# Where a second stream's steps are put among the loads of sixteen experts

## The chip, the cores and the metric

The kernel runs on one core of a Trainium2 chip. The metric is device time of one execution, in microseconds (us). In what follows TensorE does the matrix products, VectorE (DVE in the profile) and ScalarE (ACT) the elementwise work, GpSimd (POOL) some elementwise work and loads, SyncE (SP) only issues loads. PE is TensorE's matmul row in the profile, PEld its weight loads.

## The reference

The reference chains two blocks over one sequence of 256 tokens of width 1024, all in fp32. The first block is attention followed by a mixture of 16 experts; the second has two layers, and its first layer also updates a second sequence, the context, of 256 tokens. What matters here is the expert part and the context's share of the second block's first layer:

```python
def run_expert(args):                       # 16 times; each expert takes its 32 best tokens
    wg, wu, wd, ie, ge = args               # wg, wu: 1024 x 2816, wd: 2816 x 1024
    xe = h[b_rows, ie]
    he = jax.nn.silu(xe @ wg) * (xe @ wu)
    return (he @ wd) * ge[..., None].astype(h.dtype)
...
hc = ctx * (1 + csc1) + csh1                # the context, layer 0
y, yc = _mla_mixer(h, hc, ...)              # 8 heads of attention, low-rank projections
ctx = _layer_norm(alpha * ctx + cg1 * yc, ln1_g[i], ln1_b[i])
ctx = _layer_norm(alpha * ctx + cg2 * _mlp(ctx * (1 + csc2) + csh2, mlp_w1[i], mlp_w2[i]), ...)
```

The context's work does not depend on the experts' results, only the later layers need both.

## The kernel before

**Three parts.** `front` does the first attention and the routing, `experts` the sixteen experts, `tail` all that is left of the second block. The context's attention and MLP are written as a generator, `ctx_stream`, and run inside `experts`: each `next` of it issues one step (part of an attention unit, half a hidden chunk of the MLP, half of an output chunk) in the middle of the expert's own instructions. All engines take their instructions in the order in which the program issues them, so where a step is issued decides what waits behind it.

**One expert.** The 32 tokens of an expert are the stationary operand, the weights stream. For each of 8 slices k of the inner dimension, a tile of w_gate and one of w_up (1408 KB each) are taken, and 8 products each go into four banks of PSUM (L955 to L963; in the profile `egg<-wg` and `egu<-wg`, 16 instructions each). Then `Silu` and multiplications (`hh`), transposes (`eht`), copies (`hT`). Then 11 tiles of w_down (1024 KB each) are taken, and 4 products of each go into two banks `py` (L1006 to L1014, `ey<-wd`). At last `py` is copied to `ye`, and products with the routing matrix scatter it (`esc`), which VectorE adds to the result (L1022 to L1030).

**The loads.** `expert_loads` lists all 27 tiles of all experts in order; SP issues them. The class `Loader` gives a tile a buffer out of six (nine for the first expert); the next load is issued when an older tile's last product has been issued (`done`) and waits on the chip for that product. The context's weights (46 loads of up to 1024 KB) come on POOL's queue through a second loader with four buffers.

**PSUM.** There are eight banks: tag "g" has four, given out in pairs in turn (`pair`), tag "d" two, tag "c" two. Gate and up products take a pair of "g" each. `py`, the transposes `eht`, the scatter `esc` and many of the context's products take "d".

**The order around the change.** After each k, from the sixth k of the first expert on, the program issues as many context steps as a count asks for: `want` grows linearly with the number of k done, from `CTX_FROM` to all k but `CTX_LEFT`, up to `steps`. The stream itself has fewer steps than 154; when it is used up, `next` does nothing. Between the tiles of the down products no step is issued. Before the last expert's down products whatever is left is drained (L976).

Of the kernel before, what the change touches and what calls it, by code (L numbers as in the profile page):

```python
# [19 lines left out]
NE = 16  # L20
# [86 lines left out]
PROJ_PULLS = (0, 0, 1, 0, 0, 0, 0)  # L107
ADA_VECTOR = 6
WOUT_AT = (15, 16)
CTX_FROM = 5  # L110
CTX_LEFT = 16


class Loader:
# [39 lines left out]
def drain(gen):  # L154
    for _ in gen:
        pass


class Kernel:
# [764 lines left out]
    def experts(self, es, right, xs, oh, slots):  # L924
        tc, nc, a = self.tc, self.nc, self.a
        le = self.le
        xp = self.pool(es, "xe")
        self.load_tabs(1, xp, nc.gpsimd)
        xeT = xp.tile([128, 8, NE * CAP], F32, name="xeT")

        def gather(k):
            p = self.bank("d", [128, 512], "gat")
            n = 0
            for tt in range(2):
                for t in xs:
                    nc.tensor.matmul(p, t[:, tt, k * 128:k * 128 + 128], oh[:, tt], start=n == 0, stop=n == 3)
                    n += 1
            if k % 2:
                nc.vector.tensor_scalar(xeT[:, k], p, self.col("norm2", k), None, op0=OP.mult)
            else:  # L940
                nc.scalar.activation(xeT[:, k], p, AF.Copy, scale=self.col("norm2", k))
        ctx = None
        steps = 154
        got = 0

        for e in range(NE):
            ps = {n: self.pair("eg" + n[2:3]) for n in ("w_gate", "w_up")}
            if e == 0:
                gather(0)
            for k in range(8):  # L950
                if e == 0 and k < 7:
                    gather(k + 1)
                elif e == 0:
                    slots()
                for n in ("w_gate", "w_up"):  # L955
                    w = le.take((n, e, k))
                    for h in range(2):
                        for j in range(4):
                            c0 = j * FJ + h * 352
                            nc.tensor.matmul(ps[n][h][32 * j:32 * j + 32, :352],  # L960
                                             xeT[:, k, e * CAP:(e + 1) * CAP], w[:, c0:c0 + 352],
                                             start=k == 0, stop=k == 7, skip_group_check=True)
                    le.done((n, e, k))  # L963
                if (e, k) == (0, 4):
                    self.early.close()
                    ew = self.pool(es, "ew")
                    self.sw = self.rows = self.pool(es, "sw")
                    ctx = self.ctx_stream()
                if ctx is None:
                    continue  # L970
                want = steps * (8 * e + k + 1 - CTX_FROM) // (8 * NE - CTX_LEFT - CTX_FROM)
                while got < want:
                    got += 1
                    next(ctx, None)
            if e == NE - 1:
                drain(ctx)  # L976

            hh = ew.tile([128, 2, FJ], F32, name="hh", tag="hy")
            h2 = hh.rearrange("p u (a b) -> p u a b", a=2)
            for h in range(2):  # L980
                nc.scalar.activation(h2[:, 0, h], ps["w_gate"][h][:, :352], AF.Silu)
                for u in (1, 0):
                    nc.vector.tensor_mul(h2[:, u, h], h2[:, 0, h], ps["w_up"][h][:, :352])  # L983

            hT = ew.tile([128, 11, 2, 32], F32, name="hT")
            hr = hh.rearrange("p u (m r) -> p r (u m)", r=11)
            for b in range(3):
                n = (4, 4, 3)[b]
                p = self.bank("d", [128, n, 128], "eht%d" % b)
                for i in range(n):  # L990
                    nc.tensor.transpose(p[:, i], hr[:, 4 * b + i], self.ident)
                pv = p.rearrange("p r (q s t) -> p r q s t", q=2, s=2)
                for s in range(2):
                    f = nc.scalar.copy if s else nc.vector.tensor_copy
                    f(hT[64 * s:64 * s + 64, 4 * b:4 * b + n], pv[64 * s:64 * s + 64, :, :, s])
            if e < NE - 1:
                sg, ye = ew.tile([128, 256], F32, name="sg"), None
            else:
                t = self.s8([128, 2048], "sgye")
                sg, ye, jk = t[:, :256], t[:, 256:256 + D], t[:, 256 + D:768 + D]  # L1000
                nc.scalar.activation(self.warm, self.one, AF.Sqrt)
            nc.vector.tensor_scalar(sg, self.tab("iota"), self.idxg[:, e, 0:1], self.idxg[:, e, 1:2],
                                    op0=OP.is_equal, op1=OP.mult)
            py = [self.bank("d", [128, 512], "ey%d" % h) for h in range(2)]

            for n in range(11):  # L1006
                w = le.take(("d", e, n))
                for h in range(2):
                    for u in range(2):
                        r, q = (2 * (n // 2) + u, n % 2) if n < 10 else (10, u)  # L1010
                        s = 2 * u + (h + n) % 2
                        nc.tensor.matmul(py[h][32 * s:32 * s + 32, :], hT[:, r, q], w[:, u, h * 512:h * 512 + 512],  # L1012
                                         start=n < 2, stop=n >= 9, skip_group_check=True)
                le.done(("d", e, n))  # L1014
                if le.next == len(le.items) and self.lw.hold:

                    self.lw.hold = None
                    self.lw.pump()
            if ye is not None:
                return sg, ye, py, jk  # L1020
            ye = ew.tile([128, D], F32, name="ye", tag="hy")
            nc.scalar.copy(ye[:, :512], py[0])  # L1022
            nc.vector.tensor_copy(ye[:, 512:], py[1])  # L1023
            for tt in range(2):
                for h in range(2):
                    p = self.bank("d", [128, 512], "esc")
                    nc.tensor.matmul(p, sg[:, tt * 128:tt * 128 + 128], ye[:, h * 512:h * 512 + 512],
                                     start=True, stop=True)
                    xs_ = self.x[:, tt, h * 512:h * 512 + 512]
                    nc.vector.tensor_add(xs_, xs_, p)  # L1030
# [1077 lines left out]
```

## Time and profile before

| what | value |
|---|---|
| median of 3 timed runs | 2421.96 us (2421.23 to 2422.09) |
| the profiled execution's own time | 2429.35 us |
| its span, first to last instruction | 2427.5 us |
| mean granted clock of TensorE over the span | 0.87 |
| TensorE busy | 2075.3 us, 85% |
| VectorE busy | 821.8 us, 34% |
| read from memory over the span | 783.23 MB |
| up to 220 us: share of the transfer engines, GB/s | 0.85, 300 |
| 220 to 1655 us | 0.99, 410 |
| 1655 to 2427 us | 0.53, 173 |

How to read the rows of the next section. In the page's part in 40 slices a digit is the busy share of a slice of 60.7 us in tenths. In a table of stretches each row has the stretch, its length, the busy time of PE, PEld, DVE, ACT and POOL with the number of instructions, the granted clock of TensorE (1.00 is 2.4 GHz, 0.50 is 1.2 GHz), the share of time in which the 16 transfer engines were busy, and GB/s. In a timeline each row has the start, the length, engine, source line, what is written and read, the count, and in brackets how long the engine sat idle before it and what ended that. In a list of waits: who waited for whom, total us, times, longest us.

### The profile page before, as it was taken

How to read it: one execution, taken by the hardware profiler on the slowest of the kernel's cores; microseconds unless marked ns; L12 is line 12 of the kernel's file. 1: busy time of each engine (PE TensorE's matmuls, PEld its weight loads, DVE VectorE, ACT ScalarE, POOL GpSimd, SP SyncE). 2: the span in 40 equal slices, each digit the busy share in tenths (PEclk: the TensorE clock that was granted, in tenths of full speed). 3: DMA queues.
4: the chain of work that ended last, by engine and by line, in shares of the span. 5: the costliest groups of instructions: out<-in, count | busy, mean ns of one | idle time of the engine just before them, and what ended most of it. 6: DMA issues, size and time to landing. Idle time of an engine off the chain costs nothing. (4 is left out here: it accounts for less than half of the span.)

```text
span 2427.5 us, 32038 instructions
## 1 busy us (share of the span) xinstructions
PE 2075.3 (85%) x13644; PEld 1255.1 (52%) x13644; DVE 821.8 (34%) x1488; ACT 544.2 (22%) x984; POOL 246.4 (10%) x253
## 2 busy tenths in 40 slices
PE   8998888797898888987777777777998999998998
PEld 7864334332443433533122111114787998987897
DVE  5643112221112111113011001105558765377555
ACT  5432011200000000000000000004444453375443
POOL 2121000001000000000000000003213013133001
PEclk9988898897988988989666666658999999999999
DMA  9788999799999999999999999997537864333652
GB/s 336 259 316 337 410 392 422 292 417 415 411 416 416 413 404 414 414 418 392 423 422 421 422 422 422 420 423 287 204 125 257 271 221 131 101 103 131 206 185 87
DMA packets 179222, 787.59 MB, mean 324 GB/s; under 512 B 13280, under 2 KB 73928, under 8 KB 125576
## 3 DMA queue, kind: packets, MB, share of 16 engines
q1 hardware_dynamic: 154648, 694.96, 72.6%
q0 software_dynamic: 24288, 89.54, 10.2%
q8 instruction: 107, 1.75, 0.3%
q10 hardware_dynamic: 144, 1.05, 0.1%
q14 instruction: 35, 0.29, 0.0%
HBM read 783.23 MB, written 2.27 MB: 324 GB/s over the span
## 5 line engine op out<-in xcount | busy, mean ns | idle before, releaser
L1012 PE MATMUL ey<-wd,hT 128*32 128x512 f32 x1408 | 242.2, 769 | 107.2 <-DMA wd<-in_w_down 107.2
L960 PE MATMUL egu<-wg,xeT 128*32 128x352 f32 x2048 | 228.3, 574 | 61.4 <-DMA wg<-in_w_up 61.3
L378 DVE TENSOR_TENSOR wl<-cwt,wh 128x1024 fp32r<-128x1024 f32 (+1 forms) x202 | 259.9, 1329 | 58.0 <-ACT wh L377 57.8
L960 PE MATMUL egg<-wg,xeT 128*32 128x352 f32 x2048 | 224.8, 567 | 42.5 <-DMA wg<-in_w_gate 42.4
L377 ACT CAST wh<-cwt 128x1024 fp32r<-128x1024 f32 (+2 forms) x218 | 214.6, 1034 | 94.1 <-issue 50.1
L1012 PEld LDWEIGHTS ey<-wd,hT 128*32 128x32 f32 x1408 | 40.4, 123 | 290.8 <-DMA wd<-in_w_down 234.7
L960 PEld LDWEIGHTS egu<-wg,xeT 128*32 128x32 f32 x2048 | 68.4, 127 | 205.4 <-DMA wg<-in_w_up 120.7
L960 PEld LDWEIGHTS egg<-wg,xeT 128*32 128x32 f32 x2048 | 60.8, 124 | 195.3 <-issue 104.7
L173 PE MATMUL ph<-hTxh,wh 128*128 128x256 f32 x512 | 146.0, 285 | 1.5 <-ACT hTxh L1110 1.5
L174 PE MATMUL ph<-hTxl,wh 128*128 128x256 f32 x512 | 145.9, 285 | 0.7 <-DVE hTxl L1113 0.7
L175 PE MATMUL ph<-hTxh,wl 128*128 128x256 f32 x512 | 145.5, 284 | 0.8 <-DVE wl L378 0.8
L983 DVE TENSOR_TENSOR hh<-hh,egu 128x352 f32<-128x352 f32 x64 | 32.4, 519 | 300.3 <-PE egu L960 295.9
L1489 ACT ACTIVATE hu<-ph 128x512 f32<-128x512 f32 x48 | 28.7, 597 | 444.6 <-PE ph L171 340.5
L171 PE MATMUL py<-cwt,hs 128*128 128x512 f32 x256 | 121.1, 620 | 0.0
L171 PE MATMUL ph<-hcT,cwt 128*128 128x256 f32 x512 | 118.1, 385 | 0.0
L1023 DVE COPY ye<-ey 128x512 f32<-128x512 f32 x15 | 10.4, 691 | 315.3 <-PE ey L1012 315.3
L171 PEld LDWEIGHTS ph<-hcT,cwt 128*128 128x128 f32 x512 | 96.0, 191 | 27.6 <-issue 15.1
L173 PE MATMUL acc<-wh,hsh 128*128 128x512 f32 (+1 forms) x256 | 99.3, 388 | 5.9 <-ACT hsh L1497 5.9
L173 PEld LDWEIGHTS ph<-hTxh,wh 128*128 128x128 f32 x512 | 98.4, 192 | 2.7 <-ACT hTxh L1110 2.1
L174 PEld LDWEIGHTS ph<-hTxl,wh 128*128 128x128 f32 x512 | 98.3, 192 | 1.9 <-issue 0.8
L175 PEld LDWEIGHTS ph<-hTxh,wl 128*128 128x128 f32 x512 | 98.4, 192 | 1.0 <-DVE wl L378 1.0
L175 PE MATMUL acc<-wh,hsl 128*128 128x512 f32 (+1 forms) x256 | 98.6, 385 | 0.0
(545 smaller groups left out, 3454.7 us busy)
## 6 DMA issues: line engine op xcount, KB each, us to landing
wg<-in_w_gate SPq DMA_DIRECT2D x128, 1408.0 KB, 17.3
wg<-in_w_up SPq DMA_DIRECT2D x128, 1408.0 KB, 17.9
wd<-in_w_down SPq DMA_DIRECT2D x176, 1024.0 KB, 13.2
cwt<-in_w SPq DMA_DIRECT2D x64, 1024.0 KB, 5.3
cwt<-in_w POOLq DMA_DIRECT2D x32, 1024.0 KB, 14.5
adaw<-in_ada_w SPq DMA_DIRECT2D x24, 1024.0 KB, 8.0
adaw<-in_ada_w POOLq DMA_DIRECT2D x24, 1024.0 KB, 7.6
cwt<-in_w_in SPq DMA_DIRECT2D x12, 1024.0 KB, 10.5
```

The lines of the kernel that those rows point to most:

```text
L171: t.matmul(out, L[0], R[0], start=start, stop=stop, **kw)
L173: t.matmul(out, L[0], R[0], start=start, stop=False, **kw)
L174: t.matmul(out, L[0], R[1], start=False, stop=False, **kw)
L175: t.matmul(out, L[1], R[0], start=False, stop=stop, **kw)
L377: (high or nc.scalar.copy)(parts[0][:, s], t[:, s])
L378: (eng or self.low_eng).tensor_tensor(parts[1][:, s], t[:, s], parts[0][:, s].bitcast(F32), op=OP.subtract)
L960: nc.tensor.matmul(ps[n][h][32 * j:32 * j + 32, :352], xeT[:, k, e * CAP:(e + 1) * CAP], w[:, c0:c0 + 352], start=k == 0, stop=k == 7, ski ...
L983: nc.vector.tensor_mul(h2[:, u, h], h2[:, 0, h], ps["w_up"][h][:, :352])
L1012: nc.tensor.matmul(py[h][32 * s:32 * s + 32, :], hT[:, r, q], w[:, u, h * 512:h * 512 + 512], start=n < 2, stop=n >= 9, skip_group_check=True)
L1023: nc.vector.tensor_copy(ye[:, 512:], py[1])
L1489: nc.scalar.activation(u, p, AF.Relu)
```

## The change

Steps are counted in units of bytes: a k has 11 units (two tiles of 1408 KB), a tile of the down products 4 (1024 KB), an expert 8 x 11 + 11 x 4 = 132. The context starts at the same k as before (unit 55) and is dealt over the units up to the end of the fifteenth expert; 109 steps stand in place of 154 over 107 k. A helper `context` issues what is due after each k and now also after each down tile. The two banks `py` of the down products come from the pairs of tag "g" in place of tag "d".

```diff
-CTX_FROM = 5
-CTX_LEFT = 16
+UNITS = 11, 4, 8 * 11 + 11 * 4
+CTX_FROM = 5 * 11
+CTX_LEFT = 8 * 11 + 11 * 4
+CTX_STEPS = 109
...
         ctx = None
-        steps = 154
         got = 0
+
+        def context(units):
+
+            nonlocal got
+            want = CTX_STEPS * (units - CTX_FROM) // (UNITS[2] * NE - CTX_LEFT - CTX_FROM)
+            while ctx is not None and got < want:
+                got += 1
+                next(ctx, None)
...
                     ctx = self.ctx_stream()
-                if ctx is None:
-                    continue
-                want = steps * (8 * e + k + 1 - CTX_FROM) // (8 * NE - CTX_LEFT - CTX_FROM)
-                while got < want:
-                    got += 1
-                    next(ctx, None)
+                context(UNITS[2] * e + UNITS[0] * (k + 1))
             if e == NE - 1:
                 drain(ctx)
...
-            py = [self.bank("d", [128, 512], "ey%d" % h) for h in range(2)]
+            py = self.pair("ey")
 
             for n in range(11):
                 w = le.take(("d", e, n))
...
                     self.lw.pump()
+                context(UNITS[2] * e + 8 * UNITS[0] + UNITS[1] * (n + 1))
```

## Rows read from the trace of the kernel before

**Rows 1.** The page's 40 slices, the transfer engines.
```profile
DMA  9788999799999999999999999997537864333652
```
**Rows 2.** Table of stretches: two long ones of the expert stage.
```profile
530.00:1120.00 590.00, 507.95 (x2970) 231.22 (x2970) 101.90 (x170) 27.04 (x55) 38.41 (x42) 0.89 1.01 413
...
1200.00:1640.00 440.00, 320.94 (x1946) 82.66 (x1946) 38.74 (x73) 16.29 (x37) 0.00 (x0) 0.64 1.01 422
```
**Rows 3.** Table of stretches of 20 us, those with a share below 0.99.
```profile
240.00:260.00 20.00, 15.04 (x115) 6.06 (x112) 5.67 (x14) 1.98 (x5) 0.00 (x0) 0.83 0.95 384
...
340.00:360.00 20.00, 15.97 (x107) 5.51 (x98) 4.54 (x10) 3.74 (x7) 0.75 (x1) 0.91 0.87 341
...
420.00:440.00 20.00, 16.92 (x123) 12.50 (x124) 4.87 (x17) 5.58 (x18) 0.70 (x1) 1.00 0.82 317
440.00:460.00 20.00, 15.20 (x128) 9.06 (x126) 7.62 (x24) 7.07 (x18) 1.81 (x3) 0.99 0.79 295
460.00:480.00 20.00, 14.42 (x91) 4.40 (x91) 1.75 (x5) 1.05 (x3) 0.00 (x0) 0.84 0.64 257
...
840.00:860.00 20.00, 16.53 (x90) 9.24 (x88) 4.10 (x9) 2.36 (x6) 0.90 (x1) 0.83 0.94 368
...
1140.00:1160.00 20.00, 15.06 (x92) 2.98 (x91) 1.28 (x4) 0.97 (x4) 0.00 (x0) 0.77 0.85 342
```
**Rows 4.** Timeline of TensorE, 395 to 475 us.
```profile
403.81 1.39 PE L960 MATMUL egg<-wg,xeT 128*32 128x352 f32 x16
...
413.95 1.39 PE L960 MATMUL egg<-wg,xeT 128*32 128x352 f32 x16
...
431.25 1.39 PE L960 MATMUL egg<-wg,xeT 128*32 128x352 f32 x16
...
455.04 1.17 PE L1401 MATMUL mpo<-mptS,vc 128*128 128x128 f32 x8
```
**Rows 5.** Waits of SP's queue of loads, 395 to 475 us.
```profile
SPq L909 <- PE egg L960: 28.4, 3, 15.7
```
**Rows 6.** Timeline of TensorE, a tile of the second expert's down products.
```profile
361.37 1.06 PE L1012 MATMUL ey<-wd,hT 128*32 128x512 f32 x8 [1.43 <-DMA wd<-in_w_down]
```
**Rows 7.** Timeline of TensorE, 795 to 862 us, steps of the context's MLP.
```profile
798.87 3.60 PE L171 MATMUL py<-cwt,hs 128*128 128x512 f32 x8
802.40 1.39 PE L960 MATMUL egg<-wg,xeT 128*32 128x352 f32 x16
803.61 1.37 PE L960 MATMUL egu<-wg,xeT 128*32 128x352 f32 x16
...
829.01 2.57 PE L960 MATMUL egu<-wg,xeT 128*32 128x352 f32 x16 [2.98 <-DMA wg<-in_w_up]
```
**Rows 8.** Timeline of TensorE, 1100 to 1165 us, the tenth expert's transposes.
```profile
1138.05 2.96 PE L991 MATMUL eht<-tabs,hh 128*128 128x128 f32 x11 [10.31 <-DVE hh L983]
```
**Rows 9.** Groups of instructions: count, busy us, mean ns, idle before.
```profile
L1023 DVE COPY ye<-ey 128x512 f32<-128x512 f32 x15 | 10.4, 691 | 315.3 <-PE ey L1012 315.3
```
**Rows 10.** Loads by line: queue, count, size, median us from issue to landing.
```profile
cwt<-in_w POOLq DMA_DIRECT2D x32, 1024.0 KB, 14.5
```
**Rows 11.** Table of stretches of 20 us, three more of the expert stage.
```profile
800.00:820.00 20.00, 19.89 (x130) 10.54 (x132) 3.90 (x6) 0.60 (x1) 1.85 (x3) 1.00 1.01 411
...
860.00:880.00 20.00, 13.29 (x47) 3.20 (x48) 2.15 (x4) 0.59 (x1) 0.00 (x0) 0.66 1.02 423
...
1340.00:1360.00 20.00, 15.41 (x96) 3.58 (x96) 0.00 (x0) 0.00 (x0) 0.00 (x0) 0.51 1.01 423
```
**Rows 12.** Table of stretches of 5 us, 830 to 860 us.
```profile
830.00:835.00 5.00, 5.00 (x16) 1.71 (x9) 0.00 (x0) 0.00 (x0) 0.00 (x0) 0.50 0.99 398
835.00:840.00 5.00, 5.00 (x40) 2.06 (x39) 1.37 (x2) 0.00 (x0) 0.70 (x1) 0.99 1.01 418
...
850.00:855.00 5.00, 4.94 (x21) 2.63 (x25) 1.50 (x4) 1.05 (x3) 0.00 (x0) 0.50 0.92 350
855.00:860.00 5.00, 4.97 (x42) 1.11 (x34) 0.00 (x0) 0.00 (x0) 0.00 (x0) 0.94 0.81 284
```

## The prediction

> **What bounds the kernel now.** I read the page's forty slices first. The transfer engines stand at 9 tenths in every slice from the fifth to the twenty-seventh but one, which is at 7 [rows 1]: this is the expert stage, about 220 to 1650 us. After it the transfers are light. So I took the expert stage apart, and asked where the transfer engines rest in it, since nothing else can shorten a stretch that they fill.
>
> Two long stretches give the terms. From 1200 to 1640 us no context step is left: share 1.01, 422 GB/s, TensorE busy 320.94 of 440 us at a mean granted clock of 0.64 [rows 2]. From 530 to 1120 us experts and context run together: share 1.01 again, 413 GB/s, TensorE 507.95 of 590 us at 0.89. Both are full of transfers. (A share of 1.01 is what the view shows of engines that never rest.) TensorE has slack in both, but little in the second.
>
> Then I went through the stage in stretches of 20 us and kept those whose share is below 0.99: there are seven [rows 3]. Lost time is (1.01 - share) x 20 us: 1.2 at 240, 2.8 at 340, 3.8, 4.4 and 7.4 from 420 to 480, 1.4 at 840, 3.2 at 1140, together 24.2 us. That is all that any new order of the same work can win in this stage. The bytes stay the same.
>
> Why the engines rest is seen best at 403 to 460 us [rows 4]. The gate products of five k begin at 403.81, 413.95, 431.25, ... and the last context products end at 456.2: 52.4 us for five k. One k's pair of tiles is 2 x 1408 KB, 2.88 MB, or 6.8 us at 422 GB/s; five need 34 us. TensorE is the late one, because the context takes its turn in there. The queue of loads says the same: in this window SP's loads of down tiles waited 28.4 us for gate products to free a tile, once for 15.7 us [rows 5]. There are six tiles: when TensorE falls more than their worth behind, nothing can be loaded. In the down phase it is the other way round: TensorE waits for each tile, 1.43 us before products of 1.06 us, 2.49 us a tile [rows 6]. So the stage has a phase with too much for TensorE and one with too little, and six tiles can't carry the difference where the context's steps are heaviest.
>
> **The change part by part.** *The dealing.* The context stream has 108 yields (4 + 24 + 8 + 4 + 1 + 64 + 2 + 1 by the code), so a count of 109 spends it all. Before, 154 steps were dealt over 107 k: 1.44 a k, all in the gate and up phase, spent at the end of the tenth expert. After, 109 steps go over 1925 units: a k (11 units) gets 0.62, a down tile (4 units) 0.23, an expert 7.5, spent at the end of the fifteenth. The units are right by bytes: 2.88 / 1.05 MB = 2.75 = 11 / 4.
>
> TensorE's need against the transfers', at the full clock. The gate and up products of one k take 2.6 us (1.39 and 1.37, overlapping) and a step of the context's MLP 3.6 to 3.7 us [rows 7]. In the heavy attention stretch a step costs (52.4 - 5 x 2.6) / 7.2 = 5.5 us, 7.2 being 5 x 1.44. Per k that was 2.6 + 1.44 x 5.5 = 10.5 us against 6.8 of transfers; it becomes 2.6 + 0.62 x 5.5 = 6.0 us. In the MLP 2.6 + 1.44 x 3.65 = 7.9 becomes 4.9 us, against 6.8 plus about 0.8 for the context's own half load a step. In the down phase 1.06 becomes 1.06 + 0.23 x 3.65 = 1.9 us (attention: 2.3), against 2.5. TensorE is thus ahead of the transfers everywhere, and the six tiles (15 to 20 us of transfers) cover a single long step (the k from 413.95 to 431.25 held two in 17.3 - 2.6 = 14.7 us, so some 9 for the longest [rows 4]) and the pause before the down products.
>
> The rests at 340, 420 to 480 and 840 us should go, 19.8 us. The one at 1140 has another cause: the last norm of the context runs as one block on VectorE in front of the expert's, and the transposes wait 10.31 us [rows 8]. Now its two halves fall some 1.6 k, or six down tiles, apart, so I count its 3.2 us as won too. The one at 240 us lies in the first expert with its gathers; fewer context steps fall there (2 for 4), so it may lose all or nothing of 1.2; I leave it. That gives 23.0 us.
>
> *The sums in other banks.* The down sums take the pair of banks of the gate products, which are read before the transposes, and the next up products take those of the down sums. They must wait for the copies of the sums, but the scatter products ahead of them in TensorE's order wait for those already. Cost nothing, 0.7 us an expert at worst (the copy, 691 ns [rows 9]), covered anyway by the loaded tiles. The two banks freed are what lets a context step run between down tiles; its evacuation, of the same size, must be over when the scatter wants the bank: again 0.7 us an expert at most, under the same cover.
>
> *The context's loads.* The same 46 loads on POOL's queue, each asked for when an older tile is done, four tiles ahead. A tile lasts two MLP steps, so four last over an expert, 82 us (8 x 6.8 + 11 x 2.49), against 14.5 us to land [rows 10]: none is late. The rate over a long stretch is 413 GB/s with them and 422 without [rows 2]: a price of their bytes, which I keep at no change. If it were a price of the stream being alive, five more experts of it, 410 us, at 2% (422 to 413) would cost 9 us; inside the first stretch it is 411 GB/s at 800 us, among context steps, and 423 at 860, in a down phase [rows 11], which speaks against, so 0.
>
> *What may come new.* The clock. Before 829 us TensorE waited 2.98 us for a tile [rows 7]; in the next 5 us the granted clock read 0.50, the slower level, while TensorE was 5.00 of 5.00 us busy, and then 0.99. It had fallen behind, and at 850 to 860 the share fell to 0.92 and 0.81: 1.45 us lost [rows 12]. After the change TensorE is ahead of the transfers more often, so it waits and slows more often. At the slower level the gate and up products take 15.41 of 20 us [rows 11], 5.3 us a k, and a step up to 7.3. Bounds: none of these rests, or one of 1.45 us in each of the 8.6 experts that hold the MLP's 64 steps, 12.5 us. The plain cause at 850 was two steps in one k on top of it, which the new dealing rules out, so I take the near end: two of them, 3 us.
>
> Sum: 23 - 3 = 20 us won. The tail is a chain of other work that starts when the stage ends, so it moves forward whole. Against the profiled execution, 2429.35 us, that is 2409.3; it runs 7.4 us above the median of the three timed runs, so by their median 2421.96 - 20 = 2402 us.
>
> **Rivals.** *The clock takes half of it.* One rest of 1.45 us in each expert: 23 - 12.5 = 10.5 won, 2411.5 us. For it: the slower level in the down phases and everywhere from 1200 us [rows 2, 11]. Against: a step every 1.6 k leaves 2 us of slack a k at full clock.
>
> *Slower: the clock stays down and TensorE becomes the bound.* An expert with its share of context needs 8 x 2.6 + 11 x 1.06 + 7.5 x 3.65, about 60 us at full clock, plus about 10 us of waits at the turn to the down products; its transfers 38.5 MB / 413 GB/s = 93 us. It decides where 60 / clock + 10 = 93, at a mean clock of 0.72, between the 0.89 with the context and the 0.64 without. At 0.64 the expert would take 104 us, 11 more; over 8.6 experts 95 us lost, 72 with the rests won: 2494 us. Against it: a TensorE without pauses is what brought 0.99 back within 5 us at 835 [rows 12], so a lag heals itself. The Trainium skill (Perfetto Trace Analysis, section Matmul Optimizations) says that the matmul engine scales with utilization and that matmuls should be issued back to back in batches; by that rule thinning the context out is a loss, and this rival is its case. The trace agrees as far as the clock goes, 0.89 in the denser stretch and 0.64 in the thinner, but not that time was lost at 0.64: transfers were full there.
>
> *The rests only move.* The attention steps still come in lumps, or VectorE's part of a context step stands before an expert's turn to the down phase, and as much is lost elsewhere: 2422 us. Against: the lag that empties the tiles needs several heavy steps within 20 us, and they are now 1.6 k, 11 us, apart.
>
> **How the numbers follow.** All or nearly all of the 24.2 us: 0.68, 2402 us, with a range of its own from 2397 to 2407. Half: 0.18, 2411.5. Moves only: 0.07. Slower: 0.07. A difference of 0.2%, 4.8 us, is about what a measurement of this kernel tells from no change. So faster 0.86, same 0.07, slower 0.07. The range for 8 in 10: 2396 (all rests and a little of the rate) to 2414 (the half case with a bit more lost).
>
> **What would show it.** Right: in 20 us stretches the share stays at 1.0 from 260 to about 1630 us; the last context work ends near 1550; SP's waits for gate products shrink; the stage ends 20 us earlier, the tail has the same length. TensorE's mean clock in the stage lies between 0.64 and 0.89. Wrong: stretches with share under 0.95 at the slower level after 500 us (the clock), or at the turns to the down products (VectorE), or a rate under 410 GB/s at a full share over long stretches (the loads).

## The result and the profile after

The changed kernel takes 2402.19 us (median of four runs, 2398.96 to 2403.98) against 2422.03 us for the kernel before: a ratio of 0.9916, with a 95% interval from 0.9899 to 0.9934. The profiled execution took 2403.98 us, 25.4 less than that of before, which stood 7.3 above the median given here.

The first view is again the page's 40 slices, the transfer engines. The slice that stood at 7 in [rows 1] is full.

```profile
DMA  9788999999999999999999999997537864334652
```

Tables of stretches of the kernel after, columns as in [rows 2]: two long ones, then the places of 20 us where the rests were [rows 3], and all three with a share below 0.99.

```profile
530.00:1120.00 590.00, 454.07 (x2865) 183.33 (x2864) 88.58 (x160) 30.24 (x66) 26.88 (x27) 0.87 1.01 415
...
1200.00:1540.00 340.00, 264.32 (x1668) 109.42 (x1660) 57.77 (x99) 17.56 (x34) 8.80 (x12) 0.87 1.01 414
...
240.00:260.00 20.00, 15.18 (x105) 5.28 (x102) 5.89 (x14) 1.97 (x5) 0.00 (x0) 0.83 1.01 420
...
440.00:460.00 20.00, 17.45 (x102) 8.03 (x102) 5.22 (x11) 3.87 (x8) 0.00 (x0) 0.93 1.01 422
460.00:480.00 20.00, 15.27 (x126) 9.01 (x118) 2.60 (x9) 2.38 (x7) 0.71 (x1) 1.00 1.01 420
...
1060.00:1080.00 20.00, 15.92 (x81) 8.18 (x82) 4.66 (x10) 2.36 (x6) 0.90 (x1) 0.83 0.96 377
...
1340.00:1360.00 20.00, 16.83 (x79) 7.70 (x75) 4.79 (x10) 1.05 (x3) 0.70 (x1) 0.82 0.96 386
...
1440.00:1460.00 20.00, 16.15 (x104) 8.05 (x105) 3.94 (x9) 1.05 (x3) 0.00 (x0) 0.91 0.98 385
```

By the prediction's measure, (1.01 - share) x 20 us, the rests fell from 24.2 to 2.6 us. TensorE's clock, 0.89 and 0.64 in [rows 2], is 0.87 in both stretches (the second ends at 1540 us here, near the end of the context's work).

Two instructions that every version has make a ruler: the first gather product of the first expert, and ScalarE's copy of the last expert's down sums. Between them lie 1446.9 us before (208.3 to 1655.2) and 1424.1 after (208.3 to 1632.4): 22.8 us less, against 21.6 us fewer rests. What comes behind is 772.3 and 769.8 us.

How it looks on TensorE: the heaviest attention stretch of the kernel after, timeline of TensorE, columns as in [rows 4].

```profile
471.75 1.39 PE L970 MATMUL egg<-wg,xeT 128*32 128x352 f32 x16
...
481.90 1.39 PE L970 MATMUL egg<-wg,xeT 128*32 128x352 f32 x16
...
484.29 1.37 PE L970 MATMUL egg<-wg,xeT 128*32 128x352 f32 x16
487.96 1.39 PE L970 MATMUL egu<-wg,xeT 128*32 128x352 f32 x16 [2.30 <-DMA wg<-in_w_up]
...
523.47 3.64 PE L1017 MATMUL ey<-wd,hT 128*32 128x512 f32 x32
...
529.69 1.16 PE L1407 MATMUL mpo<-mptS,vc 128*128 128x128 f32 x8
530.78 2.78 PE L1017 MATMUL ey<-wd,hT 128*32 128x512 f32 x24
```

The k that begins at 471.75 has a step and lasts 10.2 us; the next, at 481.90, has none; the one after it finds its up tile not there yet and waits 2.30 us for the transfer. TensorE has caught up. And at 523.47 four down tiles are followed by attention products before the next three: work that stood in the gate and up phase before.

### The profile page after: what moved, and what is told of

Read it like the earlier page. It is cut to its first block, busy times and chain, and to the rows that moved or that the text cites. A ratio compares the mean times of both kernels' runs of the same rounds, so it can differ in the third digit from the quotient of the medians.

```text
span 2402.2 us, 32033 instructions
## 1 busy us (share of the span) xinstructions
PE 2013.8 (84%) x13644; PEld 1247.1 (52%) x13644; DVE 820.2 (34%) x1488; ACT 551.5 (23%) x990; POOL 245.2 (10%) x253
## 3 DMA queue, kind: packets, MB, share of 16 engines
q0 software_dynamic: 24288, 89.54, 10.2%
## 4 chain that ended last, share of the span: by engine, by line
PE 44%; DMA 40%; DVE 5%; ACT 2%; issue 1%; DVEq 0%; ACTq 0%; SPq 0%
DMA wg<-in_w_up 28%; DMA wd<-in_w_down 10%; PE egu L970 4%; PE ey L1017 4%; PE py L174 3%; PE acc L176 3%; PE acc L178 3%; PE acc L177 3%; PE ph L178 2%; PE ph L177 2%; PE ph L176 2%; DMA wg<-in_w_gate 2%; PE egg L970 2%; PE nqkv L176 2%; PE nqkv L177 2%; PE nqkv L178 2%
## 5 line engine op out<-in xcount | busy, mean ns | idle before, releaser
L970 PE MATMUL egu<-wg,xeT 128*32 128x352 f32 x2048 | 217.8, 551 | 115.0 <-DMA wg<-in_w_up 115.0
L1017 PE MATMUL ey<-wd,hT 128*32 128x512 f32 x1408 | 200.9, 680 | 83.0 <-DMA wd<-in_w_down 82.9
L970 PE MATMUL egg<-wg,xeT 128*32 128x352 f32 x2048 | 202.2, 518 | 63.0 <-DMA wg<-in_w_gate 63.0
L1516 DVE TENSOR_TENSOR accc<-accc,py 128x512 f32<-128x512 f32 x60 | 41.3, 688 | 282.9 <-PE py L174 282.9
L174 PE MATMUL py<-cwt,hs 128*128 128x512 f32 x256 | 131.7, 661 | 0.0
L174 PE MATMUL ph<-hcT,cwt 128*128 128x256 f32 x512 | 129.3, 409 | 0.0
L174 PEld LDWEIGHTS ph<-hcT,cwt 128*128 128x128 f32 x512 | 102.3, 206 | 43.0 <-issue 28.8
L1498 DVE SCALAR_TENSOR_TENSOR hs<-ph,hu 128x512 f32<-128x512 f32 x16 | 11.1, 692 | 297.4 <-ACT hu L1495 297.4
L307 POOL DMA_DIRECT2D cwt<-in_w x32 | 25.7, 803 | 802.8 <-PE ph L174 332.7
```

The source lines that it names most:

```text
L174: t.matmul(out, L[0], R[0], start=start, stop=stop, **kw)
L307: q.dma_start(v, src)
L970: nc.tensor.matmul(ps[n][h][32 * j:32 * j + 32, :352], xeT[:, k, e * CAP:(e + 1) * CAP], w[:, c0:c0 + 352], start=k == 0, stop=k == 7, ski ...
L1498: nc.vector.scalar_tensor_tensor(h, p, 0.0, u, op0=OP.max, op1=OP.mult)
L1516: nc.vector.tensor_add(s, s, p)
```

## The experiments

Each was run beside the kernel before on the same chip. Stage is the ruler above, and rests the sum of (1.01 - share) x 20 us over the stretches below 0.99 from 220 us to the stage's end; both are of the one profiled execution.

| run | median us | ratio to before (95%) | stage us | rests us |
|---|---|---|---|---|
| before | 2422.03 | | 1446.9 | 24.2 |
| the change | 2402.19 | 0.9916 (0.9899 to 0.9934) | 1424.1 | 2.6 |
| banks alone | 2417.66 | 0.9978 (0.9965 to 0.9991) | 1443.1 | 19.4 |
| 15 experts, k only, old banks | 2415.42 | 0.9967 (0.9952 to 0.9982) | 1439.8 | 15.0 |
| the same, new banks | 2410.53 | 0.9949 (0.9935 to 0.9963) | 1438.8 | 14.6 |
| the change, 10 experts | 2409.03 | 0.9942 (0.9927 to 0.9956) | 1431.4 | 9.4 |
| runs of 8 KB | 2390.11 | 0.9864 (0.9849 to 0.9878) | 1415.7 | 2.8 |
| runs of 2 KB | 2396.81 | 0.9890 (0.9867 to 0.9912) | 1417.5 | 1.4 |
| turn | 2400.86 | 0.9910 (0.9888 to 0.9932) | 1424.4 | 2.0 |
| turn and 2 KB | 2395.56 | 0.9889 (0.9866 to 0.9913) | 1420.8 | 4.2 |
| limit of five | 2400.22 | 0.9900 (0.9870 to 0.9930) | 1423.3 | 2.4 |
| five buffers | 2424.56 | 1.0016 (0.9995 to 1.0036) | 1446.7 | 8.8 |

The median of the kernel before in the three later sittings was 2421.83 to 2423.74 us. In the eight rows in which neither the loads' runs nor the number of buffers differ, stage less rests is 1420.9 to 1424.8 us: the rests alone account for the differences, within 4 us. In the three rows with longer runs it is 1412.9, 1416.1 and 1416.6 us.

**The banks alone** (in the kernel before):

```diff
-            py = [self.bank("d", [128, 512], "ey%d" % h) for h in range(2)]
+            py = self.pair("ey")
```

> The kernel before with the down sums in the pairs of tag g alone, dealing as before. Theory (the lag of TensorE makes the rests): nothing changes, 2422 us within 3, and the share of the transfer engines still falls at 420 to 480 us by the same 15 us or so. Rival (the banks themselves are part of the gain, since transposes, scatter and context products no longer queue for two banks): 5 to 15 us faster than before.

Some 5 us by the ratio, in an interval that leaves out 1: the theory missed it, and the rival's lowest figure is what was measured. TensorE's weight loads had a wait that went away. Waits of TensorE's weight loads in the kernel before, 220 to 1655 us: who waited for whom, us in all, times, longest.

```profile
PEld ey L1012 <- ACT hT L995: 14.8, 28, 0.7
```

The down sums took the banks that the last transposes were being copied from, so the first down product waited twice an expert for a copy of which its operands don't need the result; with banks of their own that wait is gone from the list. That is about 1 us a turn. The list alone doesn't show a gain, since the idle time without a releaser (`issue`) before the same weight loads grew from 40.0 to 104.8 us. The timelines of both runs do: at the five turns where the transfers rested before, the products of the first down tile end 0.2 to 1.4 us sooner after the first transpose. The rests are 4.8 us less in all.

**Fifteen experts, no steps between down tiles** (kernel before, old banks; then the new banks too):

```diff
-CTX_LEFT = 16
+CTX_LEFT = 8
...
-        steps = 154
+        steps = 109
```

> The kernel before with 109 steps dealt over 115 k, up to the end of the fifteenth expert, none between down tiles, sums in the old banks. Theory (what counts is that TensorE's need per k stays near the transfers' 6.8 us): 0.95 steps a k, in the attention part 2.6 + 0.95 x 5.5 = 7.8 us a k, a lag of some 8 us in an expert that the six tiles cover and the down phase gives back; nearly all of the gain, 2402 to 2407 us, rests of 3 to 7 us. Rival (the steps between down tiles make the gain): half of it or less, 2412 us or more.

> The run with 109 steps over 115 k (none between down tiles), now with the down sums in the pairs of tag g. It differs from the changed kernel only in where the steps stand. That run lost 15.0 us in rests and the banks alone took 4.9 off. Theory A (a heavy attention step costs 7.3 us, so 0.95 a k make 9.5 us against 6.8, and steps between down tiles are what relieves the k): rests near 10 us, 2408 to 2412 us. Rival B (the banks are what the wider dealing lacked): rests of 3 us, 2400 to 2404 us.

The first expectation failed: 15.0 us of rests are left, and the time is 2415. Timeline of TensorE in the run with the old banks, where most of the rests lie:

```profile
486.14 1.39 PE L960 MATMUL egg<-wg,xeT 128*32 128x352 f32 x16
...
495.88 1.39 PE L960 MATMUL egg<-wg,xeT 128*32 128x352 f32 x16
...
506.08 1.39 PE L960 MATMUL egg<-wg,xeT 128*32 128x352 f32 x16
...
515.82 1.39 PE L960 MATMUL egg<-wg,xeT 128*32 128x352 f32 x16
...
527.11 2.93 PE L991 MATMUL eht<-tabs,hh 128*128 128x128 f32 x11 [4.97 <-DVE hh L983]
```

Table of stretches of 5 us of the same run, old banks:

```profile
515.00:520.00 5.00, 4.92 (x49) 2.95 (x49) 1.47 (x5) 0.37 (x1) 1.81 (x3) 1.00 0.67 242
...
530.00:535.00 5.00, 5.00 (x31) 1.22 (x34) 0.67 (x2) 0.31 (x1) 0.00 (x0) 0.65 0.27 59
```

One step a k, and a k takes (515.82 - 486.14) / 3 = 9.9 us: an attention step costs 7.3 us, not 5.5. Dealt at 0.95 a k it asks for 9.5 us against 6.8, a lag of 2.7 us a k. The rests begin in the seventh k of this expert, and of the 8.6 us lost here 6.8 fall into the 20 us from 520 on, at the turn, where TensorE waits another 4.97 us for the expert's multiplications. With the new banks the time, 2410.5 us, is theory A's, and the rests are 14.6 us, more than its 10; the rival's 3 us are far off. So the steps between down tiles are worth 8.3 us by the medians (2410.5 to 2402.2) and 14.7 by the stage; the profiled execution of that run was the slowest of its nine.

**The change, spent by the tenth expert:**

```diff
-CTX_LEFT = 8 * 11 + 11 * 4
+CTX_LEFT = 6 * UNITS[2]
```

> The changed kernel, dealt by bytes and between down tiles too, but spent by the end of the tenth expert as before the change (11.4 steps an expert in place of 7.5). Theory: in the attention part 2.6 + 0.95 x 5.5 = 7.8 us a k against 7.1 and 1.06 + 0.34 x 5.5 = 2.9 against 2.5 a down tile, TensorE falls behind by some 10 us an expert over 3.3 experts with nothing to give it back; rests of 10 to 15 us beyond what the tiles cover, 2408 to 2415 us; the MLP part has none. Rival (where the steps stand decides, not how many an expert has): as the changed kernel, 2402 us.

2409.0 us, as the theory said, with rests just short of it: 7.4 us at 420 to 460 us, in the attention part, and 2.0 later. Dealing over the tiles of both phases, with the new banks, gives most of the gain at the old pace; the slower pace gives the last 7 us.

**The context's loads.** First each partition's 8 KB as one run:

```diff
-        mlp("c", 0, nc.gpsimd)
+        for c in range(16):
...
+                add(("c", "w1", 0, n), (8, 256), a["w1"][0][n * 64:n * 64 + 64].rearrange("r (s b) -> (r s) b", s=2).rearrange("p (a b) -> p a b", a=8), nc.gpsimd)
```

> The changed kernel, but the context's sixteen loads of its first MLP matrix take each partition's 8 KB as one run in place of eight runs of 1 KB (the values then stand in the wrong places; bytes, products and waits are the same). Theory (the rate of 414 to 416 GB/s in the stream's time against 422 without is a price of those loads' short runs): 8 to 19 us faster than the changed kernel, 2383 to 2394 us, rate near 422. Rival (price of a second queue being active): no difference, 2402 us.

2390.1 us, 12 below the change, as the theory had it; the rate rose, but not to its 422. Nearly all of the context's MLP lies between 720 and 1500 us. Tables of that stretch in the kernel after and in this run:

```profile
720.00:1500.00 780.00, 619.29 (x3836) 262.71 (x3832) 111.88 (x187) 31.57 (x66) 23.74 (x31) 0.88 1.01 415
```

```profile
720.00:1500.00 780.00, 620.24 (x3871) 265.44 (x3872) 111.82 (x188) 31.02 (x65) 18.81 (x30) 0.88 1.01 418
```

Two runs further down that keep the 1 KB loads and all six buffers, turn and limit of five, have 416 and 415 there. (From 530 to 1120 us, a stretch that begins before the MLP, the rate is 415 after the change and 419 here, but 418 in the run called turn as well.) The stage less rests, 1412.9 us, lies 8 us below the lowest of the eight versions. Something else changed together with the runs: POOL's queue has 2048 packets fewer (22240 for 24288), one packet of 8 KB for each of 16 loads and 128 partitions in place of two of 4 KB.

Then in runs of 2 KB, two tiles for two chunks:

```diff
+            for h in range(2):
+                add(("c", "w1", 0, n, h), (4, 512), self.kp(a["w1"][0], h * 512, 4, n * 512, 512), nc.gpsimd)
...
+                        c0 = c % 2 * 256 + j * 128
+                        ls = [t[:, k % 4, c0:c0 + 128] for t in halves[k // 4][0]]
```

> The changed kernel with the context's first MLP matrix loaded as halves of the inner dimension by 512 columns, so in runs of 2 KB in place of 1 KB; all results the same, two tiles are held for two chunks. The loads in single runs of 8 KB gained 12 us. Theory (a price for each run): 512 of 896 saved runs a partition and load, 12 x 0.57 = 7 us, 2393 to 2397 us. Rival (only long runs help, or the tiles held longer make steps wait for their weights): 2400 us or more.

2396.8 us, inside what the theory gave, but in an interval (0.9867 to 0.9912) that overlaps the change's (0.9899 to 0.9934). The rate from 720 to 1500 us is 419 GB/s, and the stage less rests 1416.1 us, below all eight versions as well; so the packets' size isn't all of it, for here the record has as many as with 1 KB (24288 on POOL's queue). By the ratios half of the gain of 8 KB is there at 2 KB, by the stage less rests more. That the gain grows with each saved run is not shown.

**The turn to the down products.** The step after the eighth k behind the expert's multiplications:

```diff
-                context(UNITS[2] * e + UNITS[0] * (k + 1))
+                if k < 7:
+                    context(UNITS[2] * e + UNITS[0] * (k + 1))
...
+            context(UNITS[2] * e + UNITS[0] * 8)
             hT = ew.tile([128, 11, 2, 32], F32, name="hT")
```

> The changed kernel with the context step that is due after the eighth k issued behind the Silu and the multiplications, still ahead of the transposes; TensorE's order is the same, VectorE and ScalarE do the expert's part first. Theory (the three rests that are left, 2.6 us, come from the turn to the down products, where the expert's multiplications stand behind the step's sums on VectorE): TensorE's waits for hh fall from 30 us in all to under 10, rests under 1 us, 2399 to 2401 us. Rival (the rests come from the slower clock before the turn): they stay, 2402 us.

Waits of TensorE for the multiplications, first in the kernel before from 220 to 1655 us, then from 220 to 1640 us in the kernel after and in this one:

```profile
PE eht L991 <- DVE hh L983: 41.2, 14, 10.3
```

```profile
PE eht L996 <- DVE hh L988: 30.2, 14, 3.4
```

```profile
PE eht L998 <- DVE hh L989: 12.4, 9, 1.8
```

The waits fell, though not under 10 us, and the three rests left by the change are gone; one of 2.0 us at 1520 is new, where the theory had under 1. There half of the context's last norm is due at the turn, and now stands ahead of the copies of the transposes on VectorE. Timeline of TensorE in this run:

```profile
1523.28 0.92 PE L998 MATMUL eht<-tabs,hh 128*128 128x128 f32 x3 [4.61 <-ACT hT L1002]
```

The time, 2400.9 us, can't be told from the change's. A rival to the dealing shows here. Each of the five places where the transfers rested before lies at a turn (the transposes begin at 249.8, 348.7, 460.4, 850.0 and 1138.0 us); only at the third do rests begin well ahead of it, at 430. No run moves this step in the kernel before, so how much of the 24.2 us the order at the turn alone would have won is not known. Both edits together:

> The changed kernel with both edits of before: the step after the eighth k behind the expert's multiplications, and the first MLP matrix in runs of 2 KB. Theory (the rests left and the short runs are separate prices): 2 + 5.5 us off 2402, 2393 to 2396 us. Rival (the order at the turn is worth nothing): as the 2 KB runs alone, 2397 us.

2395.6 us (2391.9 to 2402.0) is the lowest of the versions that keep the reference's computation, but not told apart from the 2 KB runs alone.

**The tiles in flight:**

```diff
-        le = Loader({"e": 6, "early": 3})
+        le = Loader({"e": 5, "early": 3})
```

> The changed kernel with five expert tiles in flight in place of six. Theory (the tiles in flight, some 15 to 20 us of transfers, cover TensorE's pauses and long steps): one tile is 2.5 to 3.4 us of cover, and each of the fifteen turns now shows a rest of 1 us or more; rests of 10 to 30 us, 2410 to 2430 us. Rival (with TensorE ahead of the transfers the cover is not used up): as the changed kernel within 3 us.

Nothing changed, and the run tells nothing: the limit moves only where the program issues a load. SP issues nothing but loads, and on the chip a load waits for the last product on its buffer, of which there still were six; SP's waits are those of the change (for gate products before loads of gate and up tiles 267.1 and 271.6 us in all). With five buffers:

```diff
-            n = le.next // 3
-            p = eg[n if n < 3 else (n - 1) % 2]
-            return p.tile([128, FF], F32, name=name, tag="e", bufs=3)
+            i = le.next
+            if 6 <= i < 9:
+                return eg[2].tile([128, FF], F32, name=name, tag="e", bufs=3)
+            i = (i if i < 6 else i - 3) % 5
+            return eg[i // 3].tile([128, FF], F32, name=name, tag="e", bufs=3 - i // 3)
```

> The changed kernel with five buffers for the expert's tiles, so that a load waits on the chip for the product five tiles earlier (in the run called five tiles the six buffers stayed, and SP's loads waited for the same products as before). Theory (the tiles in flight cover TensorE's pauses): the longest pause, a context step and the turn, some 10 us from the last tile taken, is more than is in flight when one tile of 2.5 to 3.4 us is missing; rests at most turns, 10 to 30 us in all, 2410 to 2430 us. Rival (TensorE is far enough ahead that five are enough): as the changed kernel within 3 us.

2424.6 us, as long as the kernel before. But the edit does more than was meant. In the order of loads the sixth tile now wants the first one's buffer, and SP's queue holds the seventh to ninth behind it, although their own buffers are free. So five tiles are loaded before the stage's first product, and not nine. Tables of stretches of the kernel after and of this run, then waits of SP's queue of loads in this run, 0 to 260 us:

```profile
180.00:200.00 20.00, 17.63 (x110) 13.33 (x108) 6.11 (x14) 6.49 (x17) 2.81 (x2) 1.00 0.93 369
```

```profile
180.00:200.00 20.00, 13.75 (x93) 10.00 (x91) 9.64 (x26) 9.07 (x19) 6.30 (x4) 0.91 0.32 133
```

```profile
SPq L903 <- PE egg L972: 36.3, 4, 31.6
```

Four tiles of 1408 KB are 5.77 MB, by estimate 13.9 us at the 414 GB/s that this run has from 220 to 1640 us. That much of the 22.6 us by which the stage is longer went into loads that the changed kernel has done before. Some 9 us are left for the missing buffer, of which 6.2 show as added rests. All rests of this run lie at turns; table of stretches, the two largest:

```profile
1360.00:1380.00 20.00, 17.16 (x104) 9.36 (x106) 4.09 (x9) 1.05 (x3) 0.70 (x1) 0.91 0.88 340
...
1460.00:1480.00 20.00, 17.40 (x107) 8.51 (x107) 0.92 (x3) 0.70 (x3) 0.00 (x0) 0.93 0.89 355
```

The time is the theory's, but for another reason in the main; its rests, 8.8 us, fall short of the 10, and the rival's 3 us are exceeded.

## Why the prediction was right, point by point

- *What bounds the stage.* Right. Rests fell by 21.6 us, the stage by 22.8, the time by 19.8, and over eight versions stage less rests stays within 4 us. The sum had 20. That the medians meet it within 0.2 us is luck: single runs of the changed kernel lie 5 us apart, and the terms below missed in both directions.
- *The dealing.* Right in direction and total, with one term mis-sized: a heavy attention step was put at 5.5 us, the mean over a window that ended with light ones, and it measures 7.3; the prediction's own k with two steps in 14.7 us had it. At 0.62 a k TensorE needs 2.6 + 0.62 x 7.3 = 7.1 us against 6.8, not 6.0, and in a down tile 1.06 + 0.23 x 7.3 = 2.7 against 2.5, not 2.3. So in the heaviest stretch it is level with the transfers and not ahead of them, and it is the steps between down tiles and the k without a step that keep it there. The prediction didn't weigh these apart; without steps between down tiles 15 us of rests are left.
- *The banks.* "Cost nothing" missed a gain: alone they took 4.8 us of rests and 3.8 us of stage. On top of the wider dealing the stage moved by 1.0 us and the medians by 4.9, in intervals that overlap; what they give there is unsettled. No run has steps between down tiles with the old banks, so that those steps need the banks is not shown.
- *The cover of six tiles.* Right that it is needed: with five buffers rests are 8.8 us in place of 2.6. The larger part of that run's loss is another thing, four tiles that are not loaded ahead of the stage.
- *The context's loads.* Right that five more experts of the stream cost nothing that shows within the 4 us of scatter: stage less rests is 1422.7 us before and 1421.5 after. That the lower rate is a price of these loads themselves is shown in part: longer runs brought 418 and 419 GB/s for 415 with the stream as long alive. What is missing to the 422 without the stream [rows 2] stays open.
- *The clock.* The forecast of 3 us of new rests stands beside 2.6, but its cause is not shown. They lie at turns, two of them behind a step run partly at the slower level (0.66 and 0.61 in the 5 us from 1060 and 1340); but putting VectorE's work in another order removed all three, so the order at the turn is a condition of them, and the clock alone isn't. The half-gain rival needed one in each of 8.6 experts; there were three.
- *The slower rival.* It needed a mean clock under 0.72; it was 0.87. The Trainium skill's rule (Perfetto Trace Analysis, section Matmul Optimizations), that matmuls should come back to back in batches, did not decide here: TensorE's work was thinned out in the former context stretch, where the clock went from 0.89 to 0.87, and added to the one without, where it went from 0.64 to 0.87, and the transfers set the time in both.
- *The first expert and the last norm.* The rest at 240 us, left out of the sum, went as well, and so did the one at 1140. The norm's halves fell 15 us apart, on either side of the multiplications. Timeline of VectorE after the change:

```profile
1510.73 0.69 DVE L1454 TENSOR_TENSOR accc<-accc,row 128x512 f32<-128x512 f32 x1
...
1520.25 2.25 DVE L988 TENSOR_TENSOR hh<-hh,egu 128x352 f32<-128x352 f32 x4 [3.57 <-PE egu L970]
...
1526.14 0.68 DVE L1454 TENSOR_TENSOR accc<-accc,row 128x512 f32<-128x512 f32 x1
```

- *The tail.* Right: 772.3 and 769.8 us.

## What to carry to other kernels

Where transfers fill a stage, list the stretches in which they rest: their sum is all that a new order can win, and here it gave the stage within 4 us in eight versions. Compare only versions that move the same bytes in the stage: an edit that loads less ahead of it lengthens it without a rest. Look at each rest for a turn between phases, where work of the second stream stands in front of the first one's. Deal a second stream's work in units of the bound resource over all phases of the first, also the phase in which the compute engine waits, and size the step by the heaviest run of steps and not by a mean. What is left after that lies in the transfers themselves, here 12 us with runs of 8 KB, a version that leaves the values in the wrong places, and some 5 with runs of 2 KB, in an interval that overlaps the change's.

## What was not expected of the hardware

- The rate at a full share depends on the shape of the loads: from 720 to 1500 us 415 and 416 GB/s with 16 of the context's 46 loads in runs of 1 KB, 418 and 419 with the same bytes in runs of 8 or 2 KB. The record's packets don't show runs of 1 or 2 KB: either way it has two of 4 KB a partition and load, and one of 8 KB with runs of 8 KB.
- The part before the first expert is the same code in all these versions and took 203.5 to 208.3 us in their profiled executions, and the part after the last 766.6 to 773.7. Two single executions thus differ by up to 4.8 us ahead of the stage and 7.1 behind it.
- A load whose buffer is free still waits behind one whose buffer is not: with five buffers SP's queue stood 31.6 us at the sixth load, and four tiles came into the stage late.
